# Other queues for the first small loads, the first weight piece in four loads, token statistics inside the first job, and the scan's gate in its own lane

## Chip, cores and metric

One core of one Trainium2 chip. The metric is the device time of one launch in microseconds (us). TensorE is called PE, VectorE DVE, ScalarE ACT, GpSimd POOL and SyncE SP.

## What is computed

One step of a one-layer decoder on 304 tokens: 16 learned meta tokens, a prompt of 256, and 8 samples of 4 tokens. Width 2048, 8 heads of 128, hidden width 5632, all in float32:

```
x   = LN(tokens; ln0_g, ln0_b)
q, z, v, g, B, C, xin = split(x @ w_in)                 # 2048 x 7168
f   = lb + (1 - lb) * sigmoid(z + b_f);  k = (1 - lb) * sigmoid(-(z + b_f))
S_t = diag(f_t) S_{t-1} + k_t v_t^T;     o_t = S_t^T silu(q_t)      # per head, in chunks of 64
o   = o * rsqrt(mean(o^2) + eps) * gnorm_g * silu(g)    # per-head norm and gate
y   = B * conv3(C * xin)
h   = LN(alpha * x + concat(o, y) @ w_o)
out = LN(alpha * h + (silu(h @ w_gate) * (h @ w_up)) @ w_down)
```

The states of the recurrence and of the convolution are outputs too.

## The kernel before, in words

**Products.** Each float32 product is taken as three of two rounded halves: weights `hi` and `lo`, activations `mh`/`ml` or `xh`/`xl`, products hi by high, hi by low, lo by high (L196 to L198). A weight piece is four blocks of 128 rows by 256 columns, 512 KB. SP loads it into `raw` (`load_to`, L122), ACT casts it to `hi` (L76), DVE subtracts for `lo` (L77; both are the helper `split`). Five `raw` buffers and five pairs of halves are kept.

**Jobs and ticks.** A job is 16 blocks against 256 output columns. `run_job` does for each block 2 x 3 matmuls and then calls `tick()`. The 28 jobs of `w_in` come in the order `z`, `vT`, `q`, `sg` for a pair of heads and `cb`, `xb`, `gbb` for a pair of convolution blocks. Then come `w_o`, gate and up, down.

**Side work.** Generators are put in lanes (`side`); each tick advances every lane by one step, and `yield n` lets n ticks pass. So a small matmul of side work stands at a fixed place in PE's order, between two blocks of a job. The instructions of the other engines are set by a scheduler, which may take them earlier. Operations through the wrapper `InOrder` (`vec`, `act`, `pool`, `pe`, `sync`; recorded at L58) keep the order of the program.

**The start.** The tokens lie in three tiles of rows, `xts[0]` to `xts[2]`; the third holds the last 16 prompt rows and the 32 sample rows. They are loaded by quarters of the columns (512 each): the two large tiles on SP, each followed by a weight piece; the small ones of the first two quarters, and the rows of `ln0_g` and `ln0_b` (tile `prow0`), on ACT; the small ones of the other half on POOL. Behind its loads ACT loads its table of logarithm and exponential. PE runs four idle products (`warm`) on the identity that POOL makes, transposes `prow0` (`pb`), then the token blocks (`turn`, tile `xT`), each when its rows have been centred by the mean of their first 128 columns (`centre`). `settle` multiplies by the gain and makes `mh` and `ml`. The first job (`zb`) runs on these; blocks 2 and 3 are turned at block 0, blocks 4 and 5 at block 2, and so on.

**The statistics.** The first eight jobs run on the centred, not yet normalised tokens; mean and deviation of each token are put in behind the product. DVE takes them for the two large tiles (`bn_stats`, one column quarter at every odd block); ACT sums the third tile in two passes, `row_sums`, at blocks 13 and 15. Behind the job, `lower_bounds` (with a table load through `log_exp_tables`) and `first_norm` follow: `bn_aggr`, `rstd_tok` (logarithm, exponential, Newton), 8 ticks of waiting, six matmuls that spread the result over the partitions (`rb`, L505), then the lane `normed_input`.

**The scans.** `scan_head` is one generator for each of heads 0 to 7, all in one lane. Head 0 begins at tick 96. Its steps on PE are, by ticks from its begin: `vtb` and `vsb` (transposes of v), `ktb` (15, transposes of the decayed keys `kp` and `kd`), `ab`, `so`, `kv`, `sb`, `ob` (30, the output). The rest of the generator is the norm and the gate: square, `nb` (a product with ones), logarithm, exponential, Newton, two products and a split into `mh` and `ml`. The next head begins behind that, 44 ticks after the last. Tiles `w1`, `w2`, `c`, `el`, `eq` and `kp` have one buffer each, so a new one waits for the last use of the old. `gates` runs the two Silu calls of a pair of heads and loads the logarithm table back; Silu needs a table load of its own.

Of the kernel before, what the change touches and what calls it, by code (L numbers as in the profile page):

```python
# [15 lines left out]
P = 128  # L16
# [45 lines left out]
def hybrid_step(ctx: ExitStack, tc: tile.TileContext, io):  # L62
# [54 lines left out]
    def load_to(end):  # L117
        while state["dma"] < min(len(pieces), end):
            p = state["dma"]
            w, k0, n, c0, mc = pieces[p]  # L120
            raw = wraw.tile([P, KB * MC], F32, tag="raw", name="raw")
            (sync if p <= NXC else nc.sync).dma_start(  # L122
                out=blocks(raw, p), in_=w[k0 * P : (k0 + n) * P, c0 : c0 + mc].rearrange("(k p) m -> p k m", p=P)
            )
            raws[p] = raw
            state["dma"] += 1
# [99 lines left out]

    ident = const.tile([P, P], F32, name="ident")
# [21 lines left out]
    def make_constants(e):  # L249
# [6 lines left out]
        for q in range(2):  # L256
# [4 lines left out]
                                    pattern=[[-DS, DB], [0, DS]], channel_multiplier=1)  # L261
        e.memset(bmask, 1.0)
# [24 lines left out]
    def lower_bounds():  # L287
        log_exp_tables()
# [17 lines left out]
    def newton(r, v, t):  # L306

        nc.vector.tensor_mul(out=t, in0=r, in1=r)
        nc.vector.tensor_mul(out=t, in0=t, in1=v)
        nc.vector.tensor_scalar(out=t, in0=t, scalar1=-0.5, scalar2=1.5, op0=ALU.mult, op1=ALU.add)  # L310
        nc.vector.tensor_mul(out=r, in0=r, in1=t)

    def rstd_tok(pool, mv, n, w, tag):
# [5 lines left out]
        nc.vector.tensor_scalar_add(out=v[:n], in0=mv[:n, :, 1], scalar1=LN_EPS)  # L319
        nc.scalar.activation(out=t[:n], in_=v[:n], func=AF.Ln)  # L320
        nc.scalar.activation(out=r[:n], in_=t[:n], func=AF.Exp, scale=-0.5)
        newton(r[:n], v[:n], t[:n])
        nc.vector.scalar_tensor_tensor(out=nmr[:n], in0=mv[:n, :, 0], scalar=-1.0, in1=r[:n], op0=ALU.mult, op1=ALU.mult)
# [12 lines left out]
    mv = xp.tile([P, 3, 2], F32, name="mv")  # L336
    bns = [xp.tile([P, NXC, 6], F32, name=f"bn{i}") for i in range(2)]
    s2t = xp.tile([P, 3], F32, name="s2t")


    with s0x:
        rows = [P, P, T - 2 * P]
        prows = x0p.tile([NP1, P], F32, name="prows")
# [4 lines left out]
        small = ((xts[0][:NMETA], io["meta_tokens"]), (xts[2][:NMETA], xin[2 * P - NMETA :]),  # L348
                 (xts[2][NMETA : NMETA + NS], io["x_sample"].rearrange("b t d -> (b t) d")))
# [18 lines left out]
        load_small(pool, slice(2 * XC, D))  # L368
        make_constants(pool)
# [75 lines left out]
        sums = row_sums()  # L445

        def first_rhs(k):
# [836 lines left out]
```

## Time and profile before

| | |
|---|---|
| median of 3 runs | 1412.1 us (1411.7 to 1412.73) |
| profiled execution | 1413.28 us |
| span of its trace | 1411.6 us |
| PE busy | 1390.3 us, 98% |
| DVE, ACT, POOL busy | 866.9, 607.3, 101.0 us |
| mean granted clock of TensorE | 0.99 |
| DMA | 231.14 MB, mean 164 GB/s |

The span is the time from the first to the last instruction of the profiled execution; its own time is 1.7 us longer. Busy is the share of the span in which an engine had an instruction running. A granted clock of 1.00 stands for 2.4 GHz, 0.50 for 1.2. In the page's 40 slices of 35 us PE shows 8 in the first, 6 in the last and 9 in all others.

### The profile page before, as it was taken

Reading aid. Unit: us, or ns where it says so; the run is one execution under the profiler, and the core shown is the slowest. Engines: PE = TensorE matmul, PEld = TensorE weight load, DVE = VectorE, ACT = ScalarE, POOL = GpSimd, SP = SyncE. Lnnn points to the kernel's source line nnn. Section 1 sums busy time; section 2 is a strip of 40 time slices with the busy share of each in tenths; the row PEclk is TensorE's granted clock in tenths of the full one; section 3 lists DMA queues with packets and bytes.
Section 4 is the critical chain, followed back from the end, with each engine's and each line's share of the span. In section 5 each row is a group of like instructions: output and inputs, shape, how many; then the busy total and the mean of one; then the engine's idle time right before and its main releaser. Section 6 shows DMA issues by size and latency. Waiting matters only on the chain.

```text
span 1411.6 us, 25147 instructions
## 1 busy us (share of the span) xinstructions
PE 1390.3 (98%) x10333; PEld 1372.2 (97%) x10333; DVE 866.9 (61%) x1431; ACT 607.3 (43%) x881; POOL 101.0 (7%) x161
## 2 busy tenths in 40 slices
PE   8999999999999999999999999999999999999996
PEld 6999999999999999999999999999999999999995
DVE  6997977776786888966444444444444444455444
ACT  5874546444443445434333333333333333343330
POOL 3000101111100332000000000000000000020000
PEclk8999999999999999999999999999999999999997
DMA  8656555555455555555555545555555555565541
GB/s 209 209 150 182 172 158 161 159 181 175 133 153 165 161 160 153 179 165 164 165 164 165 166 150 167 166 167 182 167 166 165 165 164 165 165 196 165 158 126 68
DMA packets 224628, 231.14 MB, mean 164 GB/s; under 512 B 7916, under 2 KB 219736, under 8 KB 224378
## 3 DMA queue, kind: packets, MB, share of 16 engines
q1 hardware_dynamic: 220608, 218.00, 50.4%
q0 software_dynamic: 3424, 10.98, 2.7%
q8 instruction: 81, 1.33, 0.4%
q10 hardware_dynamic: 480, 0.54, 0.2%
q14 instruction: 35, 0.29, 0.1%
HBM read 222.34 MB, written 7.15 MB: 163 GB/s over the span
## 4 chain that ended last, share of the span: by engine, by line
PE 94%; DVE 3%; ACT 1%; DMA 1%; issue 1%; DVEq 0%; ACTq 0%
PE u L196 7%; PE g L196 7%; PE wd L198 7%; PE g L197 7%; PE u L197 7%; PE wd L197 7%; PE u L198 7%; PE g L198 7%; PE wd L196 7%; PE wo L197 2%; PE wo L196 2%; PE wo L198 2%; PE sg L196 1%; PE q L196 1%; PE vT L196 1%; PE sg L197 1%
## 5 line engine op out<-in xcount | busy, mean ns | idle before, releaser
L77 DVE TENSOR_TENSOR lo<-raw,hi 128x1024 fp32r<-128x1024 f32 (+1 forms) x408 | 500.9, 1229 | 455.4 <-ACT hi L76 455.0
L76 ACT CAST hi<-raw 128x1024 fp32r<-128x1024 f32 (+1 forms) x408 | 420.7, 1032 | 602.0 <-PE u L197 162.6
L197 PE MATMUL wd<-al,hi 128*128 128x288 f32 x704 | 207.9, 295 | 0.0
L196 PE MATMUL wd<-ah,hi 128*128 128x288 f32 x704 | 207.8, 295 | 0.0
L198 PE MATMUL wd<-ah,lo 128*128 128x288 f32 x704 | 207.8, 295 | 0.0
L196 PE MATMUL g<-ygh,hi 128*128 128x288 f32 (+1 forms) x452 | 134.0, 296 | 0.0
L197 PE MATMUL g<-ygl,hi 128*128 128x288 f32 (+1 forms) x452 | 134.0, 296 | 0.0
L197 PE MATMUL u<-ygl,hi 128*128 128x288 f32 (+1 forms) x452 | 133.9, 296 | 0.0
L196 PE MATMUL u<-ygh,hi 128*128 128x288 f32 (+1 forms) x452 | 133.8, 296 | 0.0
L198 PE MATMUL g<-ygh,lo 128*128 128x288 f32 (+1 forms) x452 | 133.6, 296 | 0.0
L198 PE MATMUL u<-ygh,lo 128*128 128x288 f32 (+1 forms) x452 | 133.6, 296 | 0.0
L197 PEld LDWEIGHTS wd<-al,hi 128*128 128x128 f32 x704 | 132.3, 188 | 0.0
L198 PEld LDWEIGHTS wd<-ah,lo 128*128 128x128 f32 x704 | 132.2, 188 | 0.0
L196 PEld LDWEIGHTS wd<-ah,hi 128*128 128x128 f32 x704 | 132.1, 188 | 0.1
L198 PEld LDWEIGHTS u<-ygh,lo 128*128 128x128 f32 x452 | 85.4, 189 | 0.0
L198 PEld LDWEIGHTS g<-ygh,lo 128*128 128x128 f32 x452 | 85.3, 189 | 0.0
L196 PEld LDWEIGHTS g<-ygh,hi 128*128 128x128 f32 x452 | 85.3, 189 | 0.1
L197 PEld LDWEIGHTS g<-ygl,hi 128*128 128x128 f32 x452 | 85.3, 189 | 0.1
L196 PEld LDWEIGHTS u<-ygh,hi 128*128 128x128 f32 x452 | 85.3, 189 | 0.0
L197 PEld LDWEIGHTS u<-ygl,hi 128*128 128x128 f32 x452 | 85.3, 189 | 0.0
L198 PE MATMUL wo<-mh,lo 128*128 128x288 f32 x256 | 75.8, 296 | 0.0
L197 PE MATMUL wo<-ml,hi 128*128 128x288 f32 x256 | 75.7, 296 | 0.0
(460 smaller groups left out, 3205.3 us busy)
## 6 DMA issues: line engine op xcount, KB each, us to landing
raw<-in_w_in SPq DMA_DIRECT2D x112, 512.0 KB, 3.7
raw<-in_w_gate SPq DMA_DIRECT2D x88, 512.0 KB, 3.6
raw<-in_w_up SPq DMA_DIRECT2D x88, 512.0 KB, 3.6
raw<-in_w_down SPq DMA_DIRECT2D x79, 512.0 KB, 3.6
raw<-in_w_o SPq DMA_DIRECT2D x32, 512.0 KB, 3.7
s<-in_state_hgrn POOLq DMA_DIRECT2D x8, 512.0 KB, 5.5
out<-sn POOLq DMA_DIRECT2D x8, 512.0 KB, 4.5
raw<-in_w_down SPq DMA_DIRECT2D x15, 256.0 KB, 2.8
```

The source lines that it names most:

```text
L76: a.copy(out=hi, in_=src)
L77: v.tensor_tensor(out=lo, in0=src, in1=hi.bitcast(F32), op=ALU.subtract)
L196: eng.matmul(o, hi[:, i % kb, cs], xh, start=(i == 0), stop=False)
L197: eng.matmul(o, hi[:, i % kb, cs], xl, start=False, stop=False)
L198: eng.matmul(o, lo[:, i % kb, cs], xh, start=False, stop=(i == nk - 1))
```

## The change

1. The row of `ln0_g` is loaded by POOL, as its first instruction, ahead of the identity. The meta rows of the first quarter go on SP, ahead of its own. ACT issues three loads: samples, prompt tail, `ln0_b`. The small rows of the second quarter go on POOL behind the identity, those of the other half on POOL inside `make_constants`. The first weight piece comes in four loads, one a block.
2. `bn_stats` are taken at blocks 1, 3, 5, 6, 7, 9, 10, 11; the two passes of `row_sums` at blocks 9 and 10; `bn_aggr` and `rstd_tok` at block 13, in program order. The `rb` matmuls stand directly behind the job, `normed_input` is put in its lane at once, and `lower_bounds` loads no table.
3. `scan_head` ends with `ob`. Norm and gate become the generator `gated` in a lane `gate`, and the scan's lane waits `GAP = 8` ticks before the next head.

```diff
+BN_AT = (1, 3, 5, 6, 7, 9, 10, 11)
+GAP = 8
...
-            (sync if p <= NXC else nc.sync).dma_start(
-                out=blocks(raw, p), in_=w[k0 * P : (k0 + n) * P, c0 : c0 + mc].rearrange("(k p) m -> p k m", p=P)
-            )
+            src = w[k0 * P : (k0 + n) * P, c0 : c0 + mc].rearrange("(k p) m -> p k m", p=P)
+            if p:
+                (sync if p <= NXC else nc.sync).dma_start(out=blocks(raw, p), in_=src)
+            else:
+                for k in range(n):
+                    sync.dma_start(out=blocks(raw, p)[:, k], in_=src[:, k])
...
+    load_rows(pool, prow0, 0, ("ln0_g",))
     ident = const.tile([P, P], F32, name="ident")
...
     def lower_bounds():
-        log_exp_tables()
...
-        load_small(act, slice(0, XC))
-        load_rows(act, prow0, 0, ("ln0_g", "ln0_b"))
-        load_small(act, slice(XC, 2 * XC))
+        load_small(sync, slice(0, XC), small[:1])
+        load_small(act, slice(0, XC), small[1:])
+        act.dma_start(out=prow0[NB:], in_=io["ln0_b"].rearrange("(a b) -> a b", b=P))
+        off["ln0_b"] = NB
+        load_small(pool, slice(XC, 2 * XC))
         tc.keep_in_program_order(nc.scalar.preload_act_table_set("natural_log_exp_and_others"))
...
-        load_small(pool, slice(2 * XC, D))
-        make_constants(pool)
+        make_constants(pool, lambda: load_small(pool, slice(2 * XC, D)))
...
-            if i % 2:
-                vec.bn_stats(out=bns[i // 2][:, c], in_=xts[i // 2][:, c * XC : (c + 1) * XC])
-            if k in (13, 15):
+            if k in BN_AT:
+                b = BN_AT.index(k)
+                row_stats(b % 2, b // 2)
+            if k in (9, 10):
                 next(sums)
+            if k == 13:
+                for j in range(2):
+                    vec.bn_aggr(out=mv[:, j], in_=bns[j])
+                stats.extend(rstd_tok(x0p, mv, P, 3, "x"))
...
         first_job = run_job(first_rhs, T + 2, "zb", pe)
+
+        rb = [bank("rb") for _ in range(2)]
+        for b, src in zip(rb, stats):
+            for i in range(3):
+                pe.matmul(b[:, i * P : i * P + rows[i]], src[:, i : i + 1].broadcast_to([P, P]), ident[:, : rows[i]],
+                          start=True, stop=True)
...
-    def first_norm():
-
-        for i in range(2):
-            nc.vector.bn_aggr(out=mv[:, i], in_=bns[i])
-        r, nmr = rstd_tok(sp, mv, P, 3, "x")
-        yield 8
-        for dst, src in ((xr, r), (xnm, nmr)):
-            b = bank("rb")
-            for i in range(3):
-                nc.tensor.matmul(b[:, i * P : i * P + rows[i]], src[:, i : i + 1].broadcast_to([P, P]), ident[:, : rows[i]],
-                                 start=True, stop=True)
-            nc.scalar.copy(out=dst, in_=b[:, :T])
-        side("norm", normed_input())
-        yield 1
+    for dst, b in zip((xr, xnm), rb):
+        act.copy(out=dst, in_=b[:, :T])
...
         nc.tensor.matmul(ob[:, SEQ:L], os_, fold, start=False, stop=True)
+        side("gate", gated(h, ob, sg))
+        yield GAP
+
+    def gated(h, ob, sg):
...
         yield LAG
-
         sq = tl("w2", L)
...
-    side("evac", first_norm())
+    side("norm", normed_input())
...
     flush("scan")
+    flush("gate")
```

The order of the instructions at three places. On SP, from the program's begin (names of the tokens' tiles are `xt_109` and `xt_110` before, `xt_110` and `xt_111` in the change; the brackets name the landing semaphore of an earlier load that the instruction waits for; SP and ACT take the eight of them in turn). Before:

```order
L58 DMA xt_109<-in_x_prompt 112x512
L58 DMA xt_110<-in_x_prompt 128x512
L58 DMA raw<-in_w_in 128x4x256
L58 DMA xt_109<-in_x_prompt 112x512 [waits DMAHW0_49]
L58 DMA xt_110<-in_x_prompt 128x512 [waits DMAHW2_49]
L58 DMA raw<-in_w_in 128x4x256 [waits DMAHW4_49]
```

and in the change:

```order
L60 DMA xt_110<-in_meta_tokens 16x512
L60 DMA xt_110<-in_x_prompt 112x512
L60 DMA xt_111<-in_x_prompt 128x512
L60 DMA raw<-in_w_in 128x256 x2
L60 DMA raw<-in_w_in 128x256 [waits DMAHW0_49]
L60 DMA raw<-in_w_in 128x256 [waits DMAHW1_49]
L60 DMA xt_110<-in_x_prompt 112x512 [waits DMAHW2_49]
L60 DMA xt_111<-in_x_prompt 128x512 [waits DMAHW3_49]
L60 DMA raw<-in_w_in 128x4x256 [waits DMAHW4_49]
```

The loads of the second quarter of the columns now stand behind four loads of the first weight piece; the third of these waits for semaphore 0, which is that of ACT's first load (samples, first quarter).

On ACT, from its begin up to the first centring (`xt_111` before and `xt_112` in the change are the third tile of rows). Before:

```order
L58 DMA xt_109<-in_meta_tokens 16x512
L58 DMA xt_111<-in_x_prompt 16x512
L58 DMA xt_111<-in_x_sample 32x512
L58 DMA prow0_70<-in_ln_g 16x128
L58 DMA prow0_70<-in_ln_b 16x128
L58 DMA xt_109<-in_meta_tokens 16x512 [waits DMAHW1_49]
L58 DMA xt_111<-in_x_prompt 16x512 [waits DMAHW3_49]
L58 DMA xt_111<-in_x_sample 32x512 [waits DMAHW5_49,DVE_49]
L360 ACT_TABLE_LOAD
L58 ACTIVATE xt_111<-xt_111,cen 48x512 [waits DMAHW4_49,DMAHW2_49,DVE_49]
```

and in the change:

```order
L60 DMA xt_112<-in_x_sample 32x512
L60 DMA xt_112<-in_x_prompt 16x512
L60 DMA prow_70<-in_ln_b 16x128
L368 ACT_TABLE_LOAD
L60 ACTIVATE xt_112<-xt_112,cen 48x512 [waits DMAHW2_49,DMAHW0_49,DVE_49]
```

Five of the eight loads are gone from ACT, and with them the three that wait.

On DVE, the end of head 1's chain up to `kd` (`kp` and `kd` are the operands of `ktb`, `lo` is a split of a weight piece). Before:

```order
L640 TENSOR_TENSOR qp<-q,eb 128x2x2x64
L616 TENSOR_TENSOR kp<-k,el 128x2x2x64
L617 TENSOR_TENSOR el<-k,el 128x32
L618 TENSOR_TENSOR el<-k,el 128x16
L619 TENSOR_TENSOR kp<-kp,eb 128x2x64
L626 CAST kd_2001<-el 128x64
L632 TENSOR_TENSOR eq<-q,eq 128x288
L627 TENSOR_TENSOR kd_2001<-el,kd_2001 128x64
```

and in the change:

```order
L314 TENSOR_TENSOR w_1866<-eq 128x288
L627 TENSOR_TENSOR kp<-k,el 128x2x2x64
L315 TENSOR_TENSOR w_1866<-w_1866,c 128x288
L628 TENSOR_TENSOR el<-k,el 128x32
L629 TENSOR_TENSOR el<-k,el 128x16
L316 TENSOR_SCALAR w_1866<-w_1866 128x288
L630 TENSOR_TENSOR kp<-kp,eb 128x2x64
L317 TENSOR_TENSOR eq<-eq,w_1866 128x288
L637 CAST kd_1949<-el 128x64
L79 TENSOR_TENSOR lo<-raw,hi 128x1024
L751 TENSOR_TENSOR eq<-ob,eq 128x288
L638 TENSOR_TENSOR kd_1949<-el,kd_1949 128x64
```

The Newton steps of gate 0 (L314 to L317), one split and one product of the gate (L751) now stand between the parts of the chain. At head 2 DVE's order has two splits between the gate's first operation and `kd`, where it had four. On PE the scans' `vtb` stand at ticks 96, 140, 184, 228, 272, 316, 360 and 404 before, at 96, 134, 172, 210, 248, 286, 357 and 395 in the change; ACT's switches to Silu and back stand near ticks 69, 133, 245 and 357 in both.

## Rows read from the trace of the kernel before

**Rows 1.** The windows: each stretch with its bounds (us), its length, the busy time of PE, PE's weight loads, DVE, ACT and POOL with the number of instructions, the granted clock of PE, the DMA engines' busy share and GB/s.

```profile
10.00:11.00 1.00, 0.42 (x2) 0.36 (x2) 0.10 (x1) 0.66 (x1) 0.87 (x7) 0.51 1.06 274
19.00:20.00 1.00, 1.00 (x6) 0.97 (x6) 1.00 (x2) 0.00 (x0) 0.00 (x0) 0.50 1.09 330
42.00:43.00 1.00, 1.00 (x8) 1.00 (x9) 0.88 (x1) 1.00 (x3) 0.00 (x0) 1.00 0.88 287
...
372.00:373.00 1.00, 1.00 (x7) 1.00 (x6) 1.00 (x2) 0.57 (x3) 0.00 (x0) 0.50 1.01 356
375.00:376.00 1.00, 1.00 (x8) 1.00 (x7) 0.42 (x4) 0.00 (x0) 0.00 (x0) 0.88 1.00 349
...
475.00:1390.00 915.00, 915.00 (x6888) 914.45 (x6887) 484.38 (x638) 350.44 (x431) 37.04 (x43) 1.00 0.53 163
```

**Rows 2.** The waits of PE over the whole span: what waited, for what, us in total, times, longest.

```profile
PE pb L58 <- DMA prow<-in_ln_b: 3.3, 1, 3.3
PE ktb L650 <- DVE kp L619: 2.4, 2, 2.0
...
PE rb L505 <- ACT lse L301: 1.0, 1, 1.0
```

**Rows 3.** The timeline of PE, 0 to 43 us: start, us, engine, line, operation, in brackets the idle time before it and what ended it. L58 is the wrapper that records the first job.

```profile
1.43 5.83 PE L58 MATMUL warm<-ident 128*128 128x512 f32 x8 [1.43 <-POOL mv L58]
10.58 0.28 PE L58 MATMUL pb<-ident,prow 32*128 32x32 f32 x1 [3.32 <-DMA prow<-in_ln_b]
...
12.41 1.63 PE L58 MATMUL xT<-ident,xt 48*128 48x48 f32 x5 [1.14 <-ACT xt L58]
...
16.32 0.60 PE L58 MATMUL zb<-mh,hi 128*128 128x306 f32 x1
...
19.53 1.18 PE L58 MATMUL xT<-ident,xt 128*128 128x128 f32 x6
20.46 0.39 PE L58 MATMUL zb<-mh,hi 128*128 128x306 f32 x1
...
22.24 0.82 PE L58 MATMUL xT<-ident,xt 128*128 128x128 f32 x6
22.81 0.39 PE L58 MATMUL zb<-mh,hi 128*128 128x306 f32 x1
...
32.92 0.39 PE L58 MATMUL zb<-mh,hi 128*128 128x306 f32 x1
...
42.00 0.68 PE L505 MATMUL rb<-ident,xr 128*128 128x128 f32 x4 [0.98 <-ACT lse L301]
```

**Rows 4.** The timeline of ACT, 0 to 42 us, the loads that it issues (ACTq) with it.

```profile
0.81 0.43 ACTq L58 DMA_DIRECT2D xt<-in_meta_tokens  x1
...
1.73 0.44 ACTq L58 DMA_DIRECT2D xt<-in_x_sample  x1
...
9.99 0.32 ACTq L58 DMA_DIRECT2D xt<-in_x_sample  x1
10.34 1.28 ACT L360 ACT_TABLE_LOAD   x1 [10.34 <-DMA xt<-in_meta_tokens]
...
33.68 1.91 ACT L58 ACTIVATE junk<-xt 48x2048 f32<-48x2048 f32 x1
...
38.64 1.28 ACT L285 ACT_TABLE_LOAD   x1
```

**Rows 5.** The DMA view of short stretches between 0.5 and 8 us: what was loaded by which queue, number of loads, KB, us from issue to landing. The second `x_prompt` load of SP's second pair was issued at 4.55, the `raw` of the last row at 7.69.

```profile
xt<-in_meta_tokens ACTq DMA_DIRECT2D x1, 32.0 KB, 3.1
...
xt<-in_x_sample ACTq DMA_DIRECT2D x1, 64.0 KB, 5.9
...
prow<-in_ln_g ACTq DMA_DIRECT2D x1, 8.0 KB, 8.0
...
xt<-in_meta_tokens POOLq DMA_DIRECT2D x1, 64.0 KB, 5.8
...
xt<-in_x_prompt SPq DMA_DIRECT2D x1, 256.0 KB, 7.3
...
raw<-in_w_in SPq DMA_DIRECT2D x1, 512.0 KB, 6.5
```

**Rows 6.** The timeline of SP, 3 to 8 us.

```profile
3.90 1.30 SPq L58 DMA_DIRECT2D xt<-in_x_prompt  x2
7.69 0.38 SPq L58 DMA_DIRECT2D raw<-in_w_in  x1
```

**Rows 7.** The costliest groups of the page: a split's second half on DVE, number, busy us, mean ns, idle time before and its releaser.

```profile
L77 DVE TENSOR_TENSOR lo<-raw,hi 128x1024 fp32r<-128x1024 f32 (+1 forms) x408 | 500.9, 1229 | 455.4 <-ACT hi L76 455.0
```

**Rows 8.** The timelines of ACT, DVE and PE, 142 to 203 us: the table load, `kd` and `ktb` of head 1, then head 1's `ob`, `kd` and `ktb` of head 2.

```profile
143.15 1.28 ACT L285 ACT_TABLE_LOAD   x1
...
160.02 0.21 DVE L627 TENSOR_TENSOR kd<-el,kd 128x64 fp32r<-128x64 f32 x1
...
160.41 0.27 PE L651 MATMUL ktb<-ident,kd 128*128 128x128 f32 x1
...
175.60 0.38 PE L710 MATMUL ob<-at_b,vt 128*128 128x128 f32 x2
...
197.62 0.21 DVE L627 TENSOR_TENSOR kd<-el,kd 128x64 fp32r<-128x64 f32 x1
...
201.84 0.38 PE L650 MATMUL ktb<-ident,kp 128*128 128x128 f32 x2
```

More of the change, by code (lines that the diff above doesn't have):

```diff
@@ L247, in hybrid_step, with make_constants @@
     logom = const.tile([P, H], F32, name="logom")
-    def make_constants(e):
+    def make_constants(e, then):
         e.memset(cmask, 1.0)
@@ L261, in make_constants @@
                                     pattern=[[-DS, DB], [0, DS]], channel_multiplier=1)
+        then()
         e.memset(bmask, 1.0)
@@ L304, in lower_bounds, with newton @@
         nc.vector.tensor_sub(out=logom, in0=dd[:, 1], in1=lse)
[L306 to L311, printed above, removed]
+    def newton(r, v, t, e=nc.vector):
+        e.tensor_mul(out=t, in0=r, in1=r)
+        e.tensor_mul(out=t, in0=t, in1=v)
+        e.tensor_scalar(out=t, in0=t, scalar1=-0.5, scalar2=1.5, op0=ALU.mult, op1=ALU.add)
+        e.tensor_mul(out=r, in0=r, in1=t)
     def rstd_tok(pool, mv, n, w, tag):
@@ L318, in rstd_tok @@
         nmr = pool.tile([P, w], F32, tag=tag + "n", name=tag + "n")
[L319 to L323, printed above, removed]
+        vec.tensor_scalar_add(out=v[:n], in0=mv[:n, :, 1], scalar1=LN_EPS)
+        act.activation(out=t[:n], in_=v[:n], func=AF.Ln)
+        act.activation(out=r[:n], in_=t[:n], func=AF.Exp, scale=-0.5)
+        newton(r[:n], v[:n], t[:n], vec)
+        vec.scalar_tensor_tensor(out=nmr[:n], in0=mv[:n, :, 0], scalar=-1.0, in1=r[:n], op0=ALU.mult, op1=ALU.mult)
         return r, nmr
@@ L334, in hybrid_step @@
     mh, ml = mixh[:, :, :L], mixl[:, :, :L]
-    mv = xp.tile([P, 3, 2], F32, name="mv")
-    bns = [xp.tile([P, NXC, 6], F32, name=f"bn{i}") for i in range(2)]
-    s2t = xp.tile([P, 3], F32, name="s2t")
     with s0x:
         rows = [P, P, T - 2 * P]
+        mv = x0p.tile([P, 3, 2], F32, name="mv")
+        bns = [x0p.tile([P, NXC, 6], F32, name=f"bn{i}") for i in range(2)]
+        s2t = x0p.tile([P, 3], F32, name="s2t")
         prows = x0p.tile([NP1, P], F32, name="prows")
@@ L347, in hybrid_step, with load_small @@
         xin = io["x_prompt"][0]
-        small = ((xts[0][:NMETA], io["meta_tokens"]), (xts[2][:NMETA], xin[2 * P - NMETA :]),
-                 (xts[2][NMETA : NMETA + NS], io["x_sample"].rearrange("b t d -> (b t) d")))
+        small = ((xts[0][:NMETA], io["meta_tokens"]), (xts[2][NMETA : NMETA + NS], io["x_sample"].rearrange("b t d -> (b t) d")),
+                 (xts[2][:NMETA], xin[2 * P - NMETA :]))
         vec.memset(xts[2][NS : 2 * NS, XC:], 0.0)
         vec.memset(xts[2][2 * NS :, XC:], 0.0)
-        def load_small(eng, cs):
-            for dst, src in small:
+        def load_small(eng, cs, which=small):
+            for dst, src in which:
                 eng.dma_start(out=dst[:, cs], in_=src[:, cs])
-        load_small(act, slice(0, XC))
-        load_rows(act, prow0, 0, ("ln0_g", "ln0_b"))
-        load_small(act, slice(XC, 2 * XC))
+        load_small(sync, slice(0, XC), small[:1])
[3 more added lines that the diff above has]
+        load_small(pool, slice(XC, 2 * XC))
         tc.keep_in_program_order(nc.scalar.preload_act_table_set("natural_log_exp_and_others"))
@@ L445, in hybrid_step, with row_stats @@
         sums = row_sums()
+        stats = []
+        def row_stats(i, c):
+            vec.bn_stats(out=bns[i][:, c], in_=xts[i][:, c * XC : (c + 1) * XC])
         def first_rhs(k):
@@ L713, in scan_head, with tl @@
         nc.tensor.matmul(ob[:, SEQ:L], os_, fold, start=False, stop=True)
+        side("gate", gated(h, ob, sg))
+        yield GAP
+    def gated(h, ob, sg):
+        def tl(tag, n):
+            return sp.tile([P, n], F32, tag=tag, name=tag)
         yield LAG
```

## The prediction

> **What bounds the kernel now.** I first asked which engine sets the end, by the windows. From 475 to 1390 us TensorE (PE) is busy for 915.00 of 915.00 us at granted clock 1.00 [rows 1]; the change touches nothing there, and it removes no product of the large jobs. So it can only win or lose time where PE waits or runs slowly, and that is before 440 us. PE's waits [rows 2] name the places: 3.3 us for the first gain and bias rows (`pb`), 1.0 for the row statistics (`rb`), 2.4 for the scan's `ktb`, 2.0 of it in one piece. The windows then show what the waits do not: after PE stood still from 7.26 (1.43 + 5.83) to 10.58 the clock was 0.51, it was still 0.50 at 19 to 20, and after the 2.0 us at `ktb` it was 0.50 once more, at 372, and 0.88 at 375; after the 0.98 us at `rb` it stayed at 1.00 [rows 1 to 3]. A wait of 2 us here costs more than itself: about 3.8 us at 1.2 instead of 2.4 GHz, which is 1.9 us more; one of 1 us does not.
>
> Then the start, on PE's timeline [rows 3]: `pb` at 10.58, the first transposes that need the small rows at 12.41, the first product at 16.32, twelve products until 19.53 (3.21 us, half speed); the next twelve take from 20.46 to 22.24 (1.78). The first job passes block 12 at 32.92. ACT's timeline [rows 4] says why so late: ScalarE (ACT) issues eight loads first, the last at 9.99 since it waits for an earlier one to land; its table load then runs from 10.34 to 11.62, and only behind it ACT centres the rows that the transposes need.
>
> **Part 1, the loads.** A load lands 3.1 us after its issue where it is the first on ACT, 5.9 for the third, 8.0 for the gain row behind them, 5.8 for POOL's first [rows 5]. After the change ACT issues three, so at 0.43 each [rows 4] its table load ends near 3.5 and hides under the landings. The gain row goes on POOL at about 0.8 and lands at 6.6 by POOL's row; the bias row, third on ACT, at 7.6 by the 5.9, at 9.7 by the 8.0; I take the first, since it now stands ahead of most of the weights' 512 KB. The warm-up products move back by POOL's issue, 0.43 to 0.65 [rows 4, 6], and end near 7.9. So `pb` at 7.9, the transposes at 8.2 instead of 12.41. From there to the first product it was 3.9 us, most of it PE at half speed; at full speed I take 2.0: 10.2. Twelve products more: 12.0 instead of 19.53.
>
> What is late next is the second quarter of the columns. Its rows were issued by SP at 3.90 and 4.55 and landed 7.3 us later, at 11.9 [rows 5, 6]. In the new order the third quarter of the first weight piece waits on SP for a landing of ACT's first load, `x_sample`, and both second-quarter loads are queued behind it. `x_sample` lands at 3.9 by the row of the first on ACT, at 6.7 by its own row; I take the middle, 5.3. Then the last of these rows is issued near 6.8. With 7.3 us again they land at 14.1; if only the bytes ahead of them count, which are the same, at 11.9. Middle 13.0, with 0.6 for centring (0.8 from ACT's table load to the transposes now) 13.6: 5.9 earlier than 19.53. The second weight piece (issued 7.69, 6.5 to land, then cast and split, at most 1.23 each [rows 5 to 7]) allows block 4 at 16.6 against 22.81, a gain of 6.2, so it is not the limit but near it. PE stands still for 1.6 us before 13.6. That lies between the 0.98 that left the clock alone and the 2.0 that lowered it, nearer to the latter: I take a fall, and charge 1.2 of its 1.9, as PE would wait for the weights in part of it. **Sum of part 1: -4.7**; bounds -2.5 (`x_sample` as late as now, at 7.6 [rows 4, 5], and 7.3 for the rows behind it) and -6.2.
>
> A rule speaks against this part. The Trainium skill, page "DMA: Bandwidth & Descriptors", section "Issuing engines are not separate DMA queues", says that DMAs of several engines share the same 16 DMA engines, and that starting them from more engines saves only the issue time, usually small beside the transfer. By it part 1 would be a rival below; one thing speaks against it, the 3.1 of ACT's first load beside the 8.0 of its fourth [rows 5].
>
> **Part 2, the statistics.** Two passes over the sample rows, 1.91 us each on ACT [rows 4], move from the job's end into its middle. In the new order the first stands ahead of the last weight piece's cast. Nothing of it reaches PE at best, 1.9 at worst; I take **+0.7**, nearer to nothing, as that piece is needed from block 12 on only. At the end of the job the table load (38.64, 1.28 us) goes, and the `rb` products move from the next job's fifth tick to directly behind this one. Their chain (second pass, logarithm, exponential, Newton steps) ends near where it is asked for. The wait now is 0.98; the products stay. From the pass's end at 38.64 to the products at 42.00 [rows 3, 4] it is 3.4 us, without the table load 2.1; if no work of PE hides any of it, that is 1.1 more than now. I take **-0.4**, between -1.0 (wait gone) and +1.1, nearer to the first, as the second pass is moved to the middle of the job.
>
> **Part 3, the gate in its own lane.** A scan starts 8 ticks after the last scan's `ob`, not 14, while the last gate is still running. The stalls that go: 2.4 at `ktb` and 1.9 of low clock, **-4.3**. Head 6, where the 2.0 stood, starts when its `q` is there, three ticks earlier than now, but the gate before it is then long done. New waits, at an ordinary head: `ob` to `ktb` is 26.2 us now (175.60 to 201.84), and six ticks of 0.89 (twelve products, 1.78) less is 20.9; the last operand `kd` is there 22.2 after `ob` (197.83) [rows 3, 8]. That is 1.3 short, but VectorE (DVE) then has two splits of 1.23 in that stretch instead of four: room 1.1, no wait. At heads 1 and 4 ACT's table switch lies in the stretch. At head 1 the last table load ends at 144.43 and `kd` at 160.23, 0.2 ahead of its use [rows 8]; 5.3 earlier needs it near 155. The order for DVE puts the Newton steps of gate 0 and one split between the halves of `kd`. One split less stands in the way (-1.2), so up to 4.1 is missing, nothing if DVE does the rest earlier. I take 2.0 with its fall of the clock, 3.9, at one of the two heads and 1.0 at the other: +4.9. **Sum +0.6**, between -4.3 and +7.5 (twice 5.9).
>
> **Sum:** -4.7 + 0.7 - 0.4 + 0.6 = -3.8, from 1413.28 of the profiled execution to 1409.5. That execution lies 1.2 above the median of the runs, 1412.1, so I forecast **1408.3**.
>
> **Rivals.**
> *The clock stays low.* The fall near 13.6 lasts as long as the first one, until 20: for it, the 10 us of 0.5 at the start with PE partly idle; against it, the 3.8 us at 372, where PE was busy. Half of 6.4 us is lost, so part 1 gives -5.9 + 3.2 = -2.7, the sum is -1.8, 1410.3.
> *The loads do not come earlier.* The 16 DMA engines are what is full, at shares above 1 already at 10 us [rows 1], and the gain row lands after 10 us whoever issues it. Only ACT's table load and centring leave the path: transposes at 10.8 instead of 12.41, -1.6, clock as now. Sum -0.7, 1411.4. This is what the rule of the Trainium skill named above would give. For it: every load but the first took 5.8 or more [rows 5]; against it: that first load, 3.1.
> *Slower: gates and scans collide on DVE.* Nothing waits for the gate any more, so its nine operations fall into the next head's chain at each of heads 1 to 5 and 7. A 2.0 us wait with its 1.9 of low clock at four of them is 15.6 - 4.3 = +11.3, the sum +6.9, 1419.0. It decides from three such heads on (+3.0). For it: the 1.3 that the ordinary head lacks before the splits are counted, and `kd` 0.2 ahead at head 1. Against it: the reordered splits.
>
> **Chances.** Forecast 0.60, low clock 0.15, loads no earlier 0.12, collision 0.13. A measurement of this kernel can tell about 0.2%, 2.8 us, from no change: faster is below 1409.3, slower above 1414.9. The forecast is only 1.0 below the first bound and its terms are uncertain by 2 to 3, so about 0.75 of its chance is faster; with a third of the low clock's, 0.50. Slower: most of the collision, 0.12. Same 0.38. The range: down to 1403 (the best bounds of parts 1 and 3 with the other terms would be 1402), up to 1414, which takes in the first two rivals and one or two collisions.
>
> **What would show it.** In the changed profile: ACT's table load near 2.2 instead of 10.34; `pb` near 8 and first product near 10; a pause of PE near 12 that ends when the second-quarter rows land; block 12 near 28; no table load of `log_exp_tables` right behind the first job. In PE's waits: `ktb` at the second and fifth scan, not the seventh. Wrong it would be if the gain row is what `pb` waits for beyond 10 us, if the clock is 0.5 until 20 again, or if `ktb` waits at three heads or more.

## The result, and the profile after

| | before | changed |
|---|---|---|
| median of 12 runs each, us | 1412.05 (1410.59 to 1412.95) | 1415.63 (1414.34 to 1416.78) |
| ratio, 95% interval | | 1.0025 [1.0016, 1.0034] |
| profiled execution, span, us | 1413.28, 1411.6 | 1415.39, 1413.7 |
| mean granted clock | 0.99 | 0.994 |

The changed kernel is slower by 0.25%, 3.6 us by the medians, where 1408.3 was forecast. The two profiled executions lie 2.1 us apart, since that of the kernel before is 1.2 above its median and that of the changed one 0.2 below. Where the time went is seen by comparing the moments at which PE begins the same job in the two traces (changed minus before):

| job begins with | before, us | changed, us | difference |
|---|---|---|---|
| first `zb` | 16.32 | 10.36 | -5.97 |
| second job, `vT` | 37.35 | 34.51 | -2.84 |
| third job, `q` | 53.62 | 48.59 | -5.03 |
| `sg` of the second pair of heads | 120.27 | 115.21 | -5.05 |
| `wo` | 441.11 | 443.25 | +2.14 |

So the start brought 5.0 us (the `vT` row is lower because the `rb` products now stand ahead of that job), nothing more happens until 120 us, and between 120 and 441 us, where the scans run, 7.2 us are lost. After that the difference stays: the spans differ by the same 2.1.

PE's waits of the changed kernel (us in total, times, the longest), against [rows 2]:

```profile
PE ktb L661 <- DVE kp L630: 5.5, 5, 2.1
...
PE ktb L662 <- DVE kd L638: 1.7, 5, 1.0
...
PE ab L668 <- DVE eq L643: 0.9, 1, 0.9
PE zb L60 <- DVE ml L60: 0.9, 2, 0.5
```

The wait for the first gain rows, `pb`, is gone. The scan's waits have grown from 2.6 us (`kp` and `kd`) to 8.1 with `ab`. On PE's timeline they stand at six of the seven heads that follow head 0, all but head 6, which alone had a long one before:

| head | at, us | waits for `kp`, `kd`, `ab` in sum, us |
|---|---|---|
| 1 | 151.75 | 1.05 (`kd`) + 0.91 (`ab`) |
| 2 | 190.03 | 0.77 |
| 3 | 228.66 | 1.49 |
| 4 | 267.65 | 2.08 |
| 5 | 306.53 | 0.86 |
| 6 | | none |
| 7 | 407.12 | 1.00 |

The landings of some of the first loads in the changed kernel (tile, source, queue, size, us from issue to landing), against [rows 5]:

```profile
xt<-in_x_sample ACTq DMA_DIRECT2D x1, 64.0 KB, 2.4
prow<-in_ln_g POOLq DMA_DIRECT2D x1, 8.0 KB, 3.4
prow<-in_ln_b ACTq DMA_DIRECT2D x1, 8.0 KB, 3.2
xt<-in_x_prompt SPq DMA_DIRECT2D x1, 256.0 KB, 5.5
```

Each of these three small ones lands within 3.4 us, where the gain row took 8.0 and the samples 5.9. PE's timeline of the start (begin, busy us, what it waited for in brackets), against [rows 3]:

```profile
2.60 5.01 PE L60 MATMUL warm<-ident 128*128 128x512 f32 x8 [2.60 <-POOL ident masks.py:199]
7.54 0.24 PE L60 MATMUL pb<-ident,prow 32*128 32x32 f32 x1
7.72 1.33 PE L60 MATMUL xT<-ident,xt 128*128 128x128 f32 x6
...
10.36 0.39 PE L60 MATMUL zb<-mh,hi 128*128 128x306 f32 x1
...
12.88 1.01 PE L60 MATMUL xT<-ident,xt 128*128 128x128 f32 x6 [0.58 <-PE zb L60]
...
26.68 0.38 PE L60 MATMUL zb<-mh,hi 128*128 128x306 f32 x1
...
32.22 0.84 PE L60 MATMUL rb<-ident,xr 128*128 128x128 f32 x6 [0.46 <-DVE xr L60]
```

`pb` follows the idle products at once, at 7.54 instead of 10.58, and block 12 comes at 26.68 instead of 32.92. ACT's table load has moved to the front (against 10.34 in [rows 4]), and its two passes over the sample rows stand in the middle of the job:

```profile
2.20 1.28 ACT L368 ACT_TABLE_LOAD   x1 [2.20 <-issue]
...
22.92 1.90 ACT L60 ACTIVATE junk<-xt 48x2048 f32<-48x2048 f32 x1
...
26.55 2.01 ACT L60 ACTIVATE junk<-xt,s2t 48x2048 f32<-48x2048 f32 x1
28.54 0.91 ACT L60 ACTIVATE mh<-xT,pvec 128x304 fp32r<-128x304 f32 x2
```

The windows of the changed kernel (begin:end, PE, then the other engines' busy times with counts, and the granted clock third from the end), against [rows 1]:

```profile
13.00:14.00 1.00, 1.00 (x8) 0.89 (x8) 1.00 (x3) 0.62 (x2) 0.87 (x7) 1.00 1.06 181
19.00:20.00 1.00, 1.00 (x9) 1.00 (x8) 0.95 (x1) 0.83 (x3) 0.00 (x0) 1.00 1.11 343
269.00:270.00 1.00, 1.00 (x6) 1.00 (x6) 1.00 (x3) 1.00 (x4) 0.00 (x0) 0.50 0.00 0
```

The clock is 1.00 at 13 and at 19 us, where it was 0.50 at 19 before; the whole start runs at 2.4 GHz. One fall to 0.50 remains, as before, but from 269.0 to 272.4, behind the 2.08 us at head 4, instead of from 371.8 behind head 6.

What holds the scan is seen best at head 3. POOL's timeline there (begin, busy us):

```profile
224.75 3.52 POOL L641 TENSOR_TENSOR sn<-s,eb 128x1024 f32<-128x1024 f32 x1 [19.64 <-ACT eb L612]
```

And DVE's, from its last splits to the two operands that `ktb` waits for:

```profile
213.99 1.23 DVE L79 TENSOR_TENSOR lo<-raw,hi 128x1024 fp32r<-128x1024 f32 x1
...
218.34 1.22 DVE L79 TENSOR_TENSOR lo<-raw,hi 128x1024 fp32r<-128x1024 f32 x1
...
221.79 1.22 DVE L79 TENSOR_TENSOR lo<-raw,hi 128x1024 fp32r<-128x1024 f32 x1
...
224.90 1.22 DVE L79 TENSOR_TENSOR lo<-raw,hi 128x1024 fp32r<-128x1024 f32 x1
226.03 0.42 DVE L627 TENSOR_TENSOR kp<-k,el 128x256 f32<-128x256 f32 x1
226.37 1.94 DVE L628 TENSOR_TENSOR el<-k,el 128x32 f32<-128x32 f32 x1
228.24 0.16 DVE L629 TENSOR_TENSOR el<-k,el 128x16 f32<-128x16 f32 x1
228.32 0.28 DVE L630 TENSOR_TENSOR kp<-kp,eb 128x128 f32<-128x128 f32 x1
...
229.00 0.21 DVE L638 TENSOR_TENSOR kd<-el,kd 128x64 fp32r<-128x64 f32 x1
```

The product `el<-k,el` has 32 columns; its neighbour of 16 takes 0.16, and the differences of `b` over the same 32 columns before it (L617) take 0.18. Here it takes 1.94, and it ends at 228.31, where POOL's `sn` ends at 228.27. `kp` stands right behind it, and PE waits for `kp`:

```profile
206.41 0.38 PE L721 MATMUL ob<-at_b,vt 128*128 128x128 f32 x2
...
228.66 0.44 PE L661 MATMUL ktb<-ident,kp 128*128 128x128 f32 x2 [1.32 <-DVE kp L630]
```

In the changed kernel this happens at each of heads 1 to 7: one of the short instructions that make `el`, `w` and the decayed keys takes 1.91 to 1.94 us and ends within 0.06 of POOL's product, which takes 1.9 to 3.5. The kernel before has it as well. At head 6, POOL's timeline and then DVE's:

```profile
365.01 2.27 POOL L630 TENSOR_TENSOR sn<-s,eb 128x1024 f32<-128x1024 f32 x1 [23.92 <-ACT eb L601]
```

```profile
365.43 1.89 DVE L604 TENSOR_SCALAR el<-b 128x16 f32<-128x16 f32 x1
```

This one, 0.23 where nothing holds it, ends at 367.32, POOL's at 367.28. So it is at heads 1, 3, 5, 6 and 7 of the kernel before; at heads 2 and 4 a split of 1.22 stands in its place and takes 1.73 and 2.97. With 14 ticks between the heads PE waited longer than 0.6 us at head 6 alone; with 8 it does so at six heads. The theory: with six ticks less the short DVE instructions right ahead of `kp` and `kd` have no room left for this hold. Its rivals: the lane itself (gates beside scans on DVE, whatever the spacing), or the short spacing with DVE's plain amount of work, in which case taking the hold away would change little.

### The profile page after: what moved, and what is told of

It reads as the page before. It is cut to its first block, busy times and chain, and to the rows that moved or that the text cites. A ratio compares the mean times of both kernels' runs of the same rounds, so it can differ in the third digit from the quotient of the medians.

```text
span 1413.7 us, 25159 instructions
## 1 busy us (share of the span) xinstructions
PE 1388.5 (98%) x10333; PEld 1369.3 (97%) x10333; DVE 868.1 (61%) x1431; ACT 604.7 (43%) x880; POOL 106.4 (8%) x165
## 4 chain that ended last, share of the span: by engine, by line
PE 90%; DVE 7%; ACT 2%; issue 1%; POOL 0%; DVEq 0%; POOLq 0%; ACTq 0%
PE u L201 7%; PE g L201 7%; PE wd L203 7%; PE g L202 7%; PE u L202 7%; PE wd L202 7%; PE g L203 7%; PE u L203 7%; PE wd L201 7%; PE wo L202 2%; PE wo L201 2%; PE wo L203 2%; DVE lo L79 1%; PE sg L201 1%; PE vT L203 1%; PE sg L202 1%
```

## The experiments

Each was timed in turn with the kernel before, on the same chip. The ratios are to those runs of the kernel before (median 1413.64 for e1 to e4, 1412.96 for e5 to e9, 1412.56 for e10 to e13); times are medians in us.

| experiment | time | ratio, 95% interval |
|---|---|---|
| e1_no_lane | 1407.48 | 0.9959 [0.9946, 0.9971] |
| e2_lane_only | 1420.29 | 1.0046 [1.0034, 1.0059] |
| e3_gap14 | 1408.02 | 0.9964 [0.9951, 0.9976] |
| e4_sn_dve | 1405.71 | 0.9946 [0.9932, 0.9959] |
| e5_no_lane_sn_dve | 1404.32 | 0.9938 [0.9926, 0.9950] |
| e6_before_sn_dve | 1408.86 | 0.9970 [0.9959, 0.9982] |
| e7_sn_late_pool | 1405.18 | 0.9945 [0.9932, 0.9957] |
| e9_sn_half | 1409.88 | 0.9976 [0.9967, 0.9985] |
| e10_one_piece | 1408.04 | 0.9968 [0.9956, 0.9981] |
| e11_loads_only | 1406.06 | 0.9956 [0.9943, 0.9968] |
| e12_stats_only | 1413.55 | 1.0007 [0.9998, 1.0016] |
| e13_gap10 | 1409.32 | 0.9979 [0.9970, 0.9988] |

### Which part loses the time

**e1_no_lane**: the changed kernel without part 3; norm and gate stand at the end of `scan_head` again.

```diff
-        side("gate", gated(h, ob, sg))
-        yield GAP
-
-    def gated(h, ob, sg):
...
         yield LAG
...
-    flush("gate")
```

> The change without its part 3: norm and gate stand inline in the scan again, loads and statistics as changed. If the loss lies in the scans, the lead of 5.0 us that the changed trace has at the begin of the fourth job stays to the end: 1412.05 - 5.0 = 1407.0, and PE's waits at ktb are those of before, 2.6 us in all. If the early start itself is given back later (for example because normed_input now runs beside other work), the time is near 1412.

Measured: 0.9959. The waits of its scans are those of the kernel before (2.5 us at `kp`, twice, the longest 2.0; 0.2 at `kd`). It leads by 4.53 us at the third job and by 5.99 at `wo`: the 1.5 more come from the clock, which did not fall behind its wait of 2.0 us. Its windows, where the kernel before stood at 0.50 soon after (same columns as above):

```profile
367.00:368.00 1.00, 1.00 (x10) 0.98 (x10) 1.00 (x4) 0.58 (x3) 0.00 (x0) 1.00 0.88 287
368.00:369.00 1.00, 1.00 (x11) 1.00 (x10) 0.78 (x2) 0.10 (x1) 0.00 (x0) 1.00 0.56 197
```

**e2_lane_only**: the kernel before with part 3 alone, the reverse of that edit.

```diff
+        side("gate", gated(h, ob, sg))
+        yield GAP
+
+    def gated(h, ob, sg):
...
+    flush("gate")
```

> The kernel before with part 3 alone. If the scans cost what the changed trace lost between the eighth job and the w_o jobs, 7.2 us, the time is 1412.05 + 7.2 = 1419.3, with six heads waiting. If the collisions need the earlier start (other phase of ACT's casts against the scans), clearly less, 1413 to 1416.

Measured: 1.0046, at `wo` 8.09 us behind, 0.89 of it from the start, so 7.2 from the scans, as much as in the changed kernel. Its waits:

```profile
PE ktb L651 <- DVE kp L620: 5.6, 5, 2.1
...
PE ktb L652 <- DVE kd L628: 1.7, 5, 1.1
...
PE ab L658 <- DVE eq L633: 0.9, 1, 0.9
```

They are those of the changed kernel. Part 3 loses the time, with or without the other two.

**e11_loads_only**: the kernel before with part 1 alone, the first five hunks of that part.

```diff
+            if p:
+                (sync if p <= NXC else nc.sync).dma_start(out=blocks(raw, p), in_=src)
+            else:
+                for k in range(n):
+                    sync.dma_start(out=blocks(raw, p)[:, k], in_=src[:, k])
...
+    load_rows(pool, prow0, 0, ("ln0_g",))
...
+        load_small(sync, slice(0, XC), small[:1])
+        load_small(act, slice(0, XC), small[1:])
...
+        load_small(pool, slice(XC, 2 * XC))
```

> The kernel before with part 1 alone. In the changed trace block 12 of the first job came 6.2 earlier and the next job's half only 5.0, so part 2 cost about 1.2 there: alone part 1 should give 5.5 to 6.2, 1406 to 1406.6 against 1412.05. If the early start only pulls forward a wait for the statistics (rb behind ACT's passes and table load), it gives 4 or less.

Measured: 0.9956, at the third job 5.37 us ahead, at `wo` 5.54. All of the start's gain is part 1's.

**e12_stats_only**: the kernel before with part 2 alone.

```diff
+BN_AT = (1, 3, 5, 6, 7, 9, 10, 11)
...
-        log_exp_tables()
...
+            if k in (9, 10):
+                next(sums)
+            if k == 13:
...
+                stats.extend(rstd_tok(x0p, mv, P, 3, "x"))
```

> The kernel before with part 2 alone. PE is slow (1.2 GHz) until 20 us there, so ACT has more room for the two passes inside the job: the rb wait and the table load go, -0.4 by the prediction, and the passes cost between 0 and +1.2: 1411.6 to 1412.9. If ACT's passes stand in PE's way there too, 1413 or more.

Measured: 1.0007, an interval that takes in no change. In its profile the third job begins 1.92 us later than in the kernel before. ACT's second pass stands ahead of the activations' halves of the last blocks, and PE waits for `ml` twice (0.55 us here and 0.33 at 36.62):

```profile
33.26 2.00 ACT L60 ACTIVATE junk<-xt,s2t 48x2048 f32<-48x2048 f32 x1
```

```profile
34.31 0.41 PE L60 MATMUL zb<-ml,hi 128*128 128x306 f32 x1 [0.55 <-DVE ml L60]
```

Three more rows of PE's waits, from 0 to 56 us, take in the third job's begin:

```profile
PE xT L60 <- PE zb L60: 0.9, 1, 0.9
PE rb L60 <- DVE xr L60: 0.5, 1, 0.5
PE vT L200 <- DVE lo L60: 0.4, 1, 0.4
```

The two waits for `ml` make 0.9 us, that of the transposes in front of block 10 grows by 0.6 (from 0.26, which e11_loads_only, without part 2, has too), a new one for the last split costs 0.4, and the `rb` wait shrinks by 0.5. With 0.4 more at the first rows, ahead of the first product, PE stands idle for 8.95 us up to the third job instead of 7.13: 1.8 of the 1.9.

At `wo` it is 0.32 behind, since in this execution too the clock did not fall at head 6. By the ratio part 2 costs 1.0 us, at most 2.3, possibly nothing.

**e10_one_piece**: e1_no_lane with the first weight piece in one load.

```diff
-            if p:
-                (sync if p <= NXC else nc.sync).dma_start(out=blocks(raw, p), in_=src)
-            else:
-                for k in range(n):
-                    sync.dma_start(out=blocks(raw, p)[:, k], in_=src[:, k])
+            (sync if p <= NXC else nc.sync).dma_start(out=blocks(raw, p), in_=src)
```

> Parts 1 and 2 without the lane, but the first weight piece in one load of 512 KB as before. If the small rows land early because few bytes stand ahead of them (they are issued first on three queues), the four loads matter little: the first product comes when the whole piece has landed and been cast, at most 1.5 us later than 10.8, 1407.5 to 1409. If the four loads are what let the small rows through, the gain row lands near 8 us or later again, the clock falls as before, and the time is near 1411.

Measured: 0.9968 against 0.9959 for e1_no_lane, intervals that overlap: the four loads are worth 1 us or nothing. The gain row lands early here too (3.4), the first product stands at 11.18, in e1_no_lane at 10.83. So the place of the small rows brings the gain, not the split of the weights.

### The lane or the spacing

**e3_gap14**: the gate keeps its lane, the heads their old spacing.

```diff
-GAP = 8
+GAP = 14
```

> The changed kernel with GAP = 14: the gate stays in its own lane, but the scans are 44 ticks apart as before. Theory 1 (the spacing is what hurts: six ticks less room for the same chain): as without the lane, 1407.0, ktb waits 2.6. Theory 2 (the lane hurts: gate and next scan share the single buffers w2, c and eq, and the order of their use changes): 1410 or more, with waits at several heads.

Measured: 0.9964, the waits of e1_no_lane to 0.1 us. So a lane of its own costs nothing. But at this spacing the gate is done before the next head's `kp`, as in e1_no_lane: DVE takes gate 0's product `eq<-ob,eq` at 144.6 and `kp` of head 1 at 154.1, where the changed kernel has `kp` at 148.2 and the gate's product at 151.1. The loss comes with the six ticks; whether by the room that they take or by the gate that now stands beside the scan, this run does not tell. e4_sn_dve does, which keeps both.

**e13_gap10**: in between.

```diff
-GAP = 8
+GAP = 10
```

> The changed kernel with GAP = 10, so two ticks (1.7 us) more for each scan; sn on POOL in its old place. The longest wait was 2.08, most were near 1: the waits fall from 8.2 to about 0.7, the clock does not fall, and head 6 stays free of the gate before it: 1415.6 - 7.5 - 1.7 = 1406.4, better than GAP = 14 (1408.0, where the two old waits are back). If order effects on DVE rule instead of room, several waits of 1 us or more remain and it is above 1409.

Measured: 0.9979, 1409.32, more time than the 1406.4 expected and just above the 1409 named for effects of order, with a wait of 2.1 us at head 1:

```profile
PE ktb L661 <- DVE kp L630: 3.1, 3, 2.1
```

Heads 2 and 7 wait 0.6 each, as the theory has it. At head 1 another order came out: gate 0 takes the one buffer of `c` before head 1 does, and gate 0 stands behind ACT's table switch. DVE's use of it for head 1 (L606) is at 147.45, in the changed kernel at 143.32. POOL's product holds a DVE instruction of that head for 1.89 us besides. So the spacing also decides who gets a shared buffer first, which the theory of the hold did not have; how much of the 2.1 is due to it was not tested.

### POOL's product

**e4_sn_dve**: the changed kernel with `sn` taken by DVE, behind the `so` products, where it is needed next.

```diff
-        nc.gpsimd.tensor_tensor(out=sn, in0=s0, in1=ebs.broadcast_to([P, DB, P]), op=ALU.mult)
         yield 1
...
+        nc.vector.tensor_tensor(out=sn, in0=s0, in1=ebs.broadcast_to([P, DB, P]), op=ALU.mult)
         yield 1
```

> The changed kernel with the product sn = s0 * eb taken by DVE, 1.2 us, behind the so matmuls, not by POOL in the middle of the chain. Theory 3 (POOL's product holds up a DVE operation of 0.18 us for 1.8 us right ahead of kp, at every head, and the tight spacing has no room for that): the waits of 8.2 us at ktb and ab shrink to about 1, the fall of the clock goes too, 1415.6 - 7 - 1.7 = about 1407. Theory 1 (DVE has simply too much to do in the shorter period): DVE has more work than before, waits of 7 or more, 1415 or more.

Measured: 0.9946, with the heads still 38 ticks apart and the gates still beside the scans. The stretch at head 3, on DVE:

```profile
224.31 0.42 DVE L627 TENSOR_TENSOR kp<-k,el 128x256 f32<-128x256 f32 x1
224.64 0.18 DVE L628 TENSOR_TENSOR el<-k,el 128x32 f32<-128x32 f32 x1
224.75 0.17 DVE L629 TENSOR_TENSOR el<-k,el 128x16 f32<-128x16 f32 x1
224.83 0.28 DVE L630 TENSOR_TENSOR kp<-kp,eb 128x128 f32<-128x128 f32 x1
...
228.02 1.22 DVE L678 TENSOR_TENSOR sn<-s,eb 128x1024 f32<-128x1024 f32 x1
```

The same instruction takes 0.18, `kp` follows at once, and DVE does 1.22 us more work at each head without a loss. PE's waits:

```profile
PE ab L667 <- DVE eq L642: 0.6, 1, 0.6
...
PE ktb L660 <- DVE kp L630: 0.4, 1, 0.4
```

8.1 us of waits have become 1.0. It is 7.38 us ahead at `wo`. So neither the gates beside the scans nor the short spacing costs more than these 1.0 us of waits; the hold does the rest.

**e7_sn_late_pool**: `sn` stays on POOL, but its factor `ebe` is made from `ktb`, so it cannot begin before `ktb` is done.

```diff
-        nc.gpsimd.tensor_tensor(out=sn, in0=s0, in1=ebs.broadcast_to([P, DB, P]), op=ALU.mult)
...
+        ebe = sp.tile([P, DB, 1], F32, tag="ebe", name="ebe")
+        nc.vector.scalar_tensor_tensor(out=ebe, in0=ktb[:, :DB].unsqueeze(2), scalar=0.0, in1=ebs, op0=ALU.mult, op1=ALU.add)
+        nc.gpsimd.tensor_tensor(out=sn, in0=s0, in1=ebe.broadcast_to([P, DB, P]), op=ALU.mult)
```

> The changed kernel with sn still on POOL, but made to wait for ktb (DVE copies the eight decays, 0.15 us, with 0 times ktb added, and POOL multiplies by the copy). If what matters is that the hold comes ahead of kp and kd, the waits go as with sn on DVE: 1405 to 1407. If any hold of 1.8 us on DVE costs as much wherever it falls, 1412 or more, with waits at kv or ob.

Measured: 0.9945, the waits of e4_sn_dve. POOL at head 3:

```profile
228.13 1.89 POOL L680 TENSOR_TENSOR sn<-s,ebe 128x1024 f32<-128x1024 f32 x1 [24.85 <-DVE ebe L679]
```

So it is not POOL's work as such but its moment: behind `ktb`, nothing that PE waits for is held (one cast at head 2 takes 1.57, and PE doesn't wait for it). It also shows that the gain of e4_sn_dve does not hang on POOL being free.

**e9_sn_half**: half of `sn` on POOL at the old place, half on DVE behind `so`.

```diff
-        nc.gpsimd.tensor_tensor(out=sn, in0=s0, in1=ebs.broadcast_to([P, DB, P]), op=ALU.mult)
+        nc.gpsimd.tensor_tensor(out=sn[:, :4], in0=s0[:, :4], in1=ebs[:, :4].broadcast_to([P, 4, P]), op=ALU.mult)
...
+        nc.vector.tensor_tensor(out=sn[:, 4:], in0=s0[:, 4:], in1=ebs[:, 4:].broadcast_to([P, 4, P]), op=ALU.mult)
```

> The changed kernel with half of sn (four of eight sequences) on POOL at its old place, the other half on DVE behind so. Theory 3 by dose: the hold is 0.9 instead of 1.8, so each head's wait shrinks by 0.9 as far as there is one: 8.2 becomes about 2.9, no fall of the clock, about 1408.6. If the waits have another cause that the move of sn only happened to change (order on DVE), they stay above 6 or vanish altogether.

Measured: 0.9976, between the changed kernel and e4_sn_dve. The held instruction takes half as long, and so do the waits:

```profile
225.81 1.08 DVE L628 TENSOR_TENSOR el<-k,el 128x32 f32<-128x32 f32 x1
```

```profile
PE ktb L661 <- DVE kp L630: 1.7, 2, 1.2
...
PE ab L668 <- DVE eq L643: 0.9, 1, 0.9
PE ktb L662 <- DVE kd L638: 0.7, 4, 0.2
```

3.3 us of waits, between 8.1 and 1.0: the loss follows the length of the hold.

**e6_before_sn_dve**: the kernel before with that edit alone (the diff of e4_sn_dve).

> The kernel before with nothing changed but sn, taken by DVE behind the so matmuls. The two ktb waits (2.6 us) go and with them, where it happens, the fall of the clock (1.7): 1412.05 - 2.6 to - 4.3, so 1407.8 to 1409.5. If POOL's product was not what made them late, 1412 to 1413.5.

Measured: 0.9970, and the 2.0 us at head 6 are gone; 0.3 us remain at `kp`. The wait that part 3 was to take away was this hold too.

**e5_no_lane_sn_dve**: e1_no_lane with the diff of e4_sn_dve, a version that beats both kernels.

> Parts 1 and 2 of the change, scans 44 ticks apart with the gate inline, and sn taken by DVE behind the so matmuls. If POOL's hold on DVE is also what made the two waits of the kernel before (2.6 us at ktb), they go: 1407.5 - 2.6 = 1404.9, and the shorter spacing of the run before last (1405.7) brings nothing. If the spacing brings something of its own, this one is slower than 1405.7.

Measured: 0.9938, 1404.32, 8.70 us ahead at `wo`. What is left of the scans' waits is one row:

```profile
PE ktb L660 <- DVE kp L630: 0.4, 1, 0.4
```

With the hold gone, 44 ticks a head are no slower than 38 (0.9946 in e4_sn_dve): the closer spacing buys nothing in this kernel.

A version that gives the gate tiles of its own was not run, so what the shared buffers alone cost is not shown; in e4_sn_dve, which shares them, it is within the 1.0 us of waits that are left.

## Why the prediction was wrong

**Part 1, forecast -4.7: right in kind, a little too small.** e11_loads_only has -5.4 at the third job, -6.2 by its ratio (1.8 either way). `pb` came at 7.54 (7.9 forecast), the transposes at 7.72 (8.2), the first product at 10.36 (10.2). What was off is the pause for the second quarter: `x_sample` landed 2.4 after its issue, at 3.2 and not at the middle value of 5.3, the second-quarter rows of the prompt took 5.5 instead of 7.3, and PE waited 0.58 us near 12.9 instead of 1.6 before 13.6. So the fall of the clock for which 1.2 was charged did not come; block 12 at 26.68 is ahead of the 28 that was named. The rival of the clock that stays low is refuted (1.00 at 13 and 19 us), and so is that of loads that come no earlier.

The prediction rested that last rival on the Trainium skill, page "DMA: Bandwidth & Descriptors", section "Issuing engines are not separate DMA queues": starting loads from more engines saves only the issue time. No run here tests that sentence, since SP, ACT and POOL issue the loads before and after. What the runs refute is what was drawn from it: with the same bytes the gain row landed 3.4 us after its issue instead of 8.0, and part 1 alone gave a ratio of 0.9956. What changed is the place of the small rows among the large ones. The support for the rival, that every load but the first took 5.8 or more, was a misreading: it holds for the rows listed, but in the trace before ACT's second load took 3.6 and SP's first two 3.5 and 4.3.

**Part 2, forecast +0.3 in sum: too small by about 1.** e12_stats_only has 1.0007, and 1.9 us at the third job in its profile. The term of 0.7 for the ACT passes, within 0 to 1.9, was too small: the waits for `ml`, in front of block 10 and for the last split make 1.9 there, 1.6 in the changed kernel (0.9, 0.6 and 0.1). The `rb` wait fell from 1.0 to 0.5, a gain of 0.5 where 0.4 was forecast.

**Part 3, forecast +0.6: this step failed; it cost 7.2.** The old stall at head 6 did go (head 6 has no wait). The new waits at heads 1 and 4, forecast as 2.0 at one and 1.0 at the other, were 1.96 and 2.08, with a fall of the clock at head 4 only. The size is near by luck: ACT's table switch was to cause them, but it is still there in e4_sn_dve, where without POOL's product they are 0.6 and 0.4. What failed is the sentence on the ordinary head: "That is 1.3 short, but VectorE (DVE) then has two splits of 1.23 in that stretch instead of four: room 1.1, no wait." Heads 2, 3, 5 and 7 waited 0.77, 1.49, 0.86 and 1.00 us, 4.1 together. Two things were wrong in it. The sum has no term for the hold. The 22.2 us were read at head 2, one of the two heads before at which it fell on a split and cost 0.5 (1.73 instead of 1.22); in the changed kernel it falls on a short instruction ahead of `kp` and `kd` at each of these heads and costs 1.7 (1.91 to 1.94 instead of some 0.2), more than the room of 1.1. And the splits did not fall by two: at head 2, where the 22.2 was read, five lie between `ob` and `kd` before and four in the changed kernel; at head 3 there are five in both, the last four between 213.99 and 226.12. So `ob` to `kd` took 22.2 to 22.8 us at these four heads (206.41 to 229.21 at head 3), no less than the 22.2 before. e4_sn_dve and e7_sn_late_pool show that the hold decides: in e4_sn_dve, with the same numbers of splits, `ob` to `kd` takes 20.5 to 21.0 at these heads, and the 8.1 us of waits fall to 1.0.

The rival "gates and scans collide on DVE", given 0.13, came out in the place and count that it named (from three heads on; six waited), but not in its mechanism: e4_sn_dve and e7_sn_late_pool keep the gates beside the scans and have 1.0 us of waits, so what the six ticks ran into was POOL's product. Its price was too high, 1419.0, since it charged each of four heads a fall of the clock and only one came.

The waits account for 5.6 of the 7.2 us: PE is idle for 2.59 us from 120 to 441 us before, and for 8.15 in the same stretch after. In the other 1.6 PE is shown busy, but it stands at the same places: PE's stream has 11 breaks instead of 3 there. Without a break, PE takes 0.49 us from the begin of the product in front of `ktb` to that of the product behind it, and 1.17 for `ab`; at the six heads with a break it takes 1.70 to 2.57, and 2.34 for `ab` at head 1. Measured against the unbroken lengths (0.27 where two of the four `ktb` products stand alone, as at head 4), these passages are 10.6 us longer in the changed kernel and 3.4 before, which is the whole 7.2. In a full stream a product of 0.29 us begins every 0.13; ahead of a break the last one runs out alone, which counts as busy. The fall of the clock behind a wait of 2 us stands once in either profile.

Part by part, the ratios times 1412 give -6.2 for the loads, +1.0 for the statistics and +6.5 for the lane (with 1.3 to 1.8 either way), +1.3 in sum; measured were +3.5. The difference lies within what the three intervals leave.

## What to carry to other kernels

Before an interval on the critical chain is counted as work that can be packed closer, compare each instruction's duration in it with its own kind elsewhere: one of 32 columns that takes 1.94 us beside 0.18 is a wait, though the trace calls it busy; here it waited for the product of another engine that ended at the same moment. A large product on POOL belongs where nothing short on DVE is awaited, or on DVE itself, where it took 1.22 us instead of 1.9 to 3.5. Where small loads gate the first product, as at this kernel's start, issue them ahead of the large ones.

## What the runs showed of the hardware

**POOL and DVE.** While POOL multiplied 128 x 1024 elements, one DVE instruction of some 0.2 us took 1.89 to 1.94 and ended with it, at each of heads 1 to 7 of the changed kernel and at five of them before; with 128 x 512 it took 1.04 to 1.08. Other DVE instructions ran at their own length inside POOL's record, large ones (`lo` at 224.90 in 1.22 us) and short ones (at head 7 those from 403.60 to 404.93, of 0.19 to 0.46 us), and POOL's record was then longer: 3.52 and 3.34 us instead of 1.89. The Trainium skill, page "SBUF — State Buffer", section "Who interferes with whom", says that DVE and GpSimd share a pair of ports under a lock held for a whole instruction, so that whichever issues later waits, and names among those concerned DVE instructions with two inputs in SBUF, and `tensor_scalar` in some modes. The trace agrees for the short instructions of both kinds (L628 and L604 above). At head 3 `lo`, with two inputs, was not held though POOL's record begins 0.15 earlier. The ends fit the rule better than the begins: in all twelve cases the held instruction begins within 0.05 us of the moment 1.9 us ahead of POOL's end. So it looks as if POOL's longer records begin with a wait of its own behind DVE; that is read from the times, and no run tests it.

**The clock.** A wait of PE of 2.0 to 2.1 us at `ktb` lowered the granted clock from 1.00 to 0.50 for some 3.4 us in the profiles of before, the changed kernel, e2_lane_only and e11_loads_only, but not in those of e1_no_lane, e3_gap14, e10_one_piece, e12_stats_only and e13_gap10, whose longest waits are the same to 0.1 us. What decides it these runs do not show. So the 1.9 us for the fall behind a wait of 2 us, which the prediction charged as certain, come in some of these executions only; and they were read too large, since half of 3.4 us is 1.7.

**Landing times.** The five small loads that the changed kernel issues ahead of its first weights, up to 2.2 us, landed 2.1 to 3.4 us after their issue. Before, the samples, issued by ACT at 1.73, took 5.9, and the gain row, at 2.20 behind eight other loads, 8.0 [rows 4, 5].
